# Read-out tables of an S5 layer formed beside the attention and kept in DRAM, with fixed bias buffers and gate stores on another queue

## The chip, the cores and the metric

The kernel runs on one core of a Trainium2 chip. The metric is the device time of one execution in microseconds (us). The engines are TensorE (PE in the profile; its weight loads are PEld), VectorE (DVE), ScalarE (ACT), GpSimd (POOL) and SyncE (SP), which here only issues transfers. Each engine works through its own instructions in order.

## What is computed

A backbone of two layers over 256 latent tokens with a prefix of 256 context tokens, width 1024, float32. In each layer one input projection feeds three token mixers and three gates:

```
h  = rms_norm(x) * (1.0 + sc1) + sh1
hc = rms_norm(ctx) * (1.0 + csc1) + csh1
u, rk, rv, nk, nv, rq, rg, nq, gates = split_cols(h @ w_in[l], IN_SPLIT)
y_s5, y_s5_c = s5_mixer(u, cu, ...)
y_ret, y_ret_c = retention_mixer(...)
y_na = neighborhood_attention(heads(nq), heads(nk), heads(nv), k_na_c, v_na_c, na_rpb[l])
x = x + g1 * merge_branches(y_s5, y_ret, y_na, gates, ...)
...
x = x + g2 * swiglu(rms_norm(x) * (1.0 + sc2) + sh2, ...)
```

Layer 0 does all of this for both streams (512 tokens), layer 1 for the latent tokens. The S5 mixer is a state space model with 32 groups of 16 channels and 64 complex states per group, in both directions. What matters here is its read-out:

```
jnp.einsum('ghp,blgp->blgh', c_re, x_re) - jnp.einsum('ghp,blgp->blgh', c_im, x_im)
```

## The kernel before

**Weights.** The weights stream from DRAM in chunks of 512 KB, in the order in which they are needed (`wraw`, L375, issued by SyncE into four raw buffers). ScalarE casts each chunk to a rounded copy (L385), VectorE subtracts this copy from the chunk and so gets the rest (L386), and each product of the network is three matmuls, L391 to L393 (`mm3`; L875 to L877 for the modulation). These are called weight matmuls below; 24 of them belong to a 128-column piece of weights over 512 tokens.

**Layer 0 around the change.** `weave` runs one generator as the main one and steps the others between its pieces, and so writes the program in an interleaved order; the scheduler of the framework then fixes the order on each engine. Buffers come from a hand-managed arena `F` that hands out space round robin, or from its top on request, so the arena's state decides what a new buffer overwrites and waits for. The sequence is: the attention's projections of the first half with the S5 input side; those of the second half with the S5 scan (`s5_scan`), the attention of the first half (`attn`) and modulation; then the gates with the attention of the second half; then, after the swap buffer is freed, more gates with the S5 read-out (`s5_out`); then the branch projections and retention, which begins with transposes at L1543.

**The S5 parts.** A sequence is cut into 32 chunks of 16 tokens. The scan runs on GpSimd over the states between chunks: 63 steps, each of two products (L1101) and two sums (L1104, L1105) on 128 x 64 elements, each step depending on the one before. Its tail exchanges two halves of the states through the buffer `swap`: two transfers on GpSimd's queue (L1111, L1112) and two copies (L1113, L1114).

The read-out needs tables per block of 8 groups, four blocks in a layer. `_prods` forms g on VectorE with six instructions over 128 x 1152 elements (L747, L748 products, L749 sum; twice, once per direction). `s5_kwin` multiplies g on TensorE by a window (L1158, called KWIN below, 16 matmuls), copies and corrects the result (L1162 to L1167) and stores it to DRAM as kws (L1171); `s5_t` loads it back in another layout as T, with four transfers (L1145). Then 48 matmuls (L1223, called OUT below) give the output: a third of them multiply by T and two thirds, with the scanned states, by g. Layer 0 does all of this inside `s5_out`; layer 1 forms its tables early, beside the FFN of layer 0 (`s5_kwins`), keeps g in DRAM as gsp and loads g and T back block by block (`s5_back`).

**Attention.** Scores, softmax, transposed scores (L1382, copied from PSUM by L1406 on ScalarE), values (L1410). Each head pair loads two bias tables (L1392), which ScalarE negates (L1393), into buffers from the arena.

**Gates.** TensorE forms a gate tile, ScalarE takes its tanh (L1668), and GpSimd's queue stores it to DRAM as tgs (L1671); SyncE loads it back later (L1687).

## Time and profile before

| | |
|---|---|
| median of three executions | 1570.82 us (1569.39 to 1572.18) |
| profiled execution: its time, its span | 1570.71 us, 1568.9 us |
| TensorE busy | 1500.3 us (96% of the span) |
| VectorE, ScalarE, GpSimd busy | 980.2, 631.9, 235.4 us |
| mean granted TensorE clock | 0.978 of full |
| read from and written to DRAM | 225.96 and 16.12 MB |

TensorE stands still for less than 5% of the span; its busy time also holds stretches in which the granted clock is at its lower level. An engine's idle time costs nothing unless TensorE waits for that engine, directly or through a chain.

### The profile page before, as it was taken

The page shows a single profiled execution, that of the slowest core. Times are in us where ns is not written, and L with a number is a line of the kernel's source. Part 1 is how long each engine was busy: PE and PEld are TensorE (multiplying, and loading weights), DVE is VectorE, ACT ScalarE, POOL GpSimd, SP SyncE. Part 2 cuts the span into 40 slices and gives each one's busy share as a digit, 9 for nine tenths or more (in the row PEclk, how much of TensorE's full clock was granted, in tenths as well). Part 3 has the DMA queues.
Part 4 walks back from the last instruction along what each step waited for, and adds up shares of the span by engine and source line. Part 5 has one row for each costly group of instructions (what it writes and reads, how often), then busy time and mean ns, then how long its engine had stood idle before and what let it go on. Part 6 is the DMA issues. An engine that isn't in the chain of part 4 may idle for free.

```text
span 1568.9 us, 25526 instructions
## 1 busy us (share of the span) xinstructions
PE 1500.3 (96%) x10066; PEld 1273.3 (81%) x10066; DVE 980.2 (62%) x1729; ACT 631.9 (40%) x1139; POOL 235.4 (15%) x620
## 2 busy tenths in 40 slices
PE   7899999969999999999999999999998999999997
PEld 6776677748887888787887788898777999899997
DVE  6683435466445587587699973732654776666566
ACT  4544444213522334332332322444644345453443
POOL 5205782000000000000000000006991000000000
PEclk9999999989999999999999999999999999999999
DMA  9423345644333323454565562432223786555552
GB/s 372 145 88 108 102 151 180 209 152 144 122 112 95 125 93 122 162 187 142 166 225 196 204 199 64 168 102 80 93 91 112 241 294 202 201 176 187 175 186 97
DMA packets 78584, 245.91 MB, mean 157 GB/s; under 512 B 9088, under 2 KB 22912, under 8 KB 76672
## 3 DMA queue, kind: packets, MB, share of 16 engines
q1 hardware_dynamic: 76864, 237.92, 46.3%
q0 software_dynamic: 1600, 6.36, 1.3%
q8 instruction: 79, 1.29, 0.3%
q14 instruction: 41, 0.34, 0.1%
HBM read 225.96 MB, written 16.12 MB: 154 GB/s over the span
## 4 chain that ended last, share of the span: by engine, by line
PE 70%; issue 8%; POOL 8%; DMA 7%; DVE 4%; ACT 1%; SPq 1%; POOLq 0%; DVEq 0%; ACTq 0%
PE psall L391 20%; PE psall L393 20%; PE psall L392 19%; DMA fa<-in_wst_dram 4%; POOL fa L1101 3%; POOL fa L1105 2%; POOL fa L1104 1%; PE psall L524 1%; PE psall L875 1%; PE psall L876 1%; DMA fa<-in_nabias_dram 1%; PE psall L877 1%; PE psall L1223 1%; PE psall L1582 1%; DMA fa<-fa 1%
## 5 line engine op out<-in xcount | busy, mean ns | idle before, releaser
L391 PE MATMUL psall<-ra 128*128 128x256 f32 (+1 forms) x2122 | 713.9, 340 | 9.3 <-DVE fa L1164 3.2
L393 PE MATMUL psall<-ra 128*128 128x256 f32 (+1 forms) x2122 | 707.6, 336 | 2.9 <-DVE ra L386 2.9
L392 PE MATMUL psall<-ra 128*128 128x256 f32 (+1 forms) x2122 | 710.1, 336 | 0.0
L386 DVE TENSOR_TENSOR ra<-fa,ra 128x1024 fp32r<-128x1024 f32 (+1 forms) x284 | 342.9, 1210 | 295.0 <-ACT ra L385 287.4
L385 ACT CAST ra<-fa 128x1024 fp32r<-128x1024 f32 (+1 forms) x284 | 293.7, 1037 | 560.6 <-PE psall L392 326.2
L391 PEld LDWEIGHTS psall<-ra 128*128 128x128 f32 x2122 | 402.7, 191 | 67.1 <-issue 11.7
L393 PEld LDWEIGHTS psall<-ra 128*128 128x128 f32 x2122 | 404.5, 191 | 46.9 <-DVE ra L386 3.9
L392 PEld LDWEIGHTS psall<-ra 128*128 128x128 f32 x2122 | 405.3, 191 | 39.8 <-issue 1.1
L1101 POOL TENSOR_TENSOR fa<-fa 128x64 f32<-128x64 f32 x252 | 87.4, 368 | 137.9 <-ACT fa L1069 128.3
L1050 POOL MEMSET fa<- 128x32 f32 x2 | 0.3, 126 | 691.0 <-DVE ra L834 691.0
L568 DVE SCALAR_TENSOR_TENSOR fa<-fa 128x1024 f32<-128x1024 f32 x70 | 87.2, 1277 | 9.2 <-DMA fa<-in_wst_dram 9.0
L875 PE MATMUL psall<-ra 128*128 128x512 f32 x192 | 78.4, 422 | 4.1 <-ACT ra L833 3.8
L876 PE MATMUL psall<-ra 128*128 128x512 f32 x192 | 77.5, 404 | 3.8 <-DVE ra L386 3.8
L877 PE MATMUL psall<-ra 128*128 128x512 f32 x192 | 74.1, 402 | 0.0
L1706 DVE SCALAR_TENSOR_TENSOR fa<-psall,fa 128x256 f32<-128x256 f32 x96 | 43.0, 477 | 46.4 <-PE psall L393 46.0
L875 PEld LDWEIGHTS psall<-ra 128*128 128x128 f32 x192 | 43.7, 230 | 13.0 <-ACT ra L833 4.9
L1105 POOL TENSOR_TENSOR fa<-fa 128x64 f32<-128x64 f32 x126 | 52.6, 417 | 9.8
L876 PEld LDWEIGHTS psall<-ra 128*128 128x128 f32 x192 | 44.5, 232 | 9.3 <-DVE ra L386 4.4
L1104 POOL TENSOR_TENSOR fa<-fa 128x64 f32<-128x64 f32 x126 | 48.0, 381 | 0.0
L877 PEld LDWEIGHTS psall<-ra 128*128 128x128 f32 x192 | 43.3, 232 | 5.6 <-issue 0.2
L748 DVE TENSOR_TENSOR fa<-fa 128x1024 f32<-128x1024 f32 (+1 forms) x32 | 40.2, 1283 | 7.2 <-DMA fa<-in_s5c_dram 7.2
L407 ACT CAST ra<-fa 128x512 fp32r<-128x512 f32 (+1 forms) x52 | 26.5, 509 | 44.6 <-DVE fa L1772 32.1
(244 smaller groups left out, 1409.4 us busy)
## 6 DMA issues: line engine op xcount, KB each, us to landing
fa<-in_wst_dram SPq DMA_DIRECT2D x364, 512.0 KB
fa<-in_wst_dram SPq DMA_DIRECT2D x16, 384.0 KB
gsp<-fa SPq DMA_DIRECT2D x4, 1152.0 KB
fa<-gsp SPq DMA_DIRECT2D x4, 1152.0 KB
xsp<-fa SPq DMA_DIRECT2D x2, 2048.0 KB
tgs<-fa POOLq DMA_DIRECT2D x16, 256.0 KB, 4.2
fa<-kws SPq DMA_DIRECT2D x32, 128.0 KB
fa<-tgs SPq DMA_DIRECT2D x16, 256.0 KB
```

Source lines behind the costliest of these rows:

```text
L385: nc.scalar.copy(hi[:, :n], t[:, :n])
L386: nc.vector.tensor_tensor(out=lo[:, :n], in0=t[:, :n], in1=hi[:, :n].bitcast(F32), op=ALU.subtract)
L391: mm(out, wh, xh, start=start, stop=False)
L392: mm(out, wh, xl, start=False, stop=False)
L393: mm(out, wl, xh, start=False, stop=stop)
L568: nc.vector.scalar_tensor_tensor(out=acc[s].ap, in0=t, scalar=c, in1=acc[s].ap, op0=ALU.mult, op1=ALU.add)
L875: mm(o, xh, hi[:, ws], start=(kk == 0), stop=False)
L876: mm(o, xh, lo[:, ws], start=False, stop=False)
L877: mm(o, xl, hi[:, ws], start=False, stop=(kk == 7))
L1101: e.tensor_tensor(out=t[:, i], in0=at(pf, pr), in1=tab[:, i * 64:(i + 1) * 64].rearrange("p (r d g) -> p r d g", r=2, d=2), op=ALU.mult)
L1104: e.tensor_tensor(out=at(cf, cr), in0=at(cf, cr), in1=t[:, 0], op=ALU.add)
L1105: e.tensor_tensor(out=at(cf, cr), in0=at(cf, cr), in1=mk(T[s % 2], 96, [[-32, 2], [16, 2], [1, 16]]), op=ALU.add)
```

## The change

Layer 0's tables are formed as layer 1's already are. `s5_kwins(0, True)` takes one buffer of 4480 columns from the arena's top, makes a small arena of its own in it, and forms g and the window there; it is woven into the second half of the attention's projections and the gates that follow. g goes to DRAM (gsp has eight tiles now) and `s5_out` of both layers loads g and T back. Four bias buffers of 384 columns are taken from the top for the whole attention of a layer. The gate stores move from GpSimd's queue to ScalarE's.

```diff
@@ layer 0
+            kw = self.s5_kwins(0, True)
             e_in = chain(*(g for blk in range(4) for g in (self.s5_e(0, b2, blk), self.s5_in(0, blk))))
             weave(self.m_na(l, 0, na), (e_in, 3))
             self.log_gamma(self.s5in[:, 192:208])
-            weave(self.m_na(l, 1, na), (self.s5_scan(l), 18), (self.attn(l, 0, na), 4), (self.take(ada, 5), 1))
-            weave(self.gates(l, 0, None), (self.attn(l, 1, na), 1.6), (self.take(ada, 5), 0.5))
+            weave(self.m_na(l, 1, na), (self.s5_scan(l), 18), (self.attn(l, 0, na), 4), (self.take(ada, 5), 1),
+                  (self.take(kw, 4), 1))
+            weave(self.gates(l, 0, None), (self.attn(l, 1, na), 1.6), (self.take(ada, 5), 0.5), (kw, 0.5))
             self.swap.free()
             weave(self.gates(l, 2, None), (self.s5_out(l, self.yslot[1]), 2), (self.take(ada, 5), 0.5))
@@ s5_kwins
-    def s5_kwins(self, l):
-
-        nc = self.nc
+    def s5_kwins(self, l, own=False):
+
+        nc, F = self.nc, self.F
+        if own:
+
+            buf = F.alloc(4480, "kwins", top=True)
+            F = Arena(buf.ap, 4480, "kwins")
         for blk in range(4):
-            gb, gv = self.s5_g(l, blk)
-            yield
-            self.s5_kwin(l, blk, gv)
-            nc.sync.dma_start(self.gsp[blk], gb.ap)
+            gb, gv = self.s5_g(l, blk, F)
+            yield
+            self.s5_kwin(l, blk, gv, F)
+            nc.sync.dma_start(self.gsp[l * 4 + blk], gb.ap)
             gb.free()
             yield
+        if own:
+            buf.free()
@@ s5_out
-        back = self.s5_back(0) if last else None
+        back = self.s5_back(l, 0)
         for blk in range(4):
-            if last:
-                gb, T = back
-                gv = self.g_view(gb)
-                back = self.s5_back(blk + 1) if blk < 3 else None
-                yield
-            else:
-                gb, gv = self.s5_g(l, blk)
-                yield
-                self.s5_kwin(l, blk, gv)
-                yield
-                T = F.alloc(1024, "T")
-                self.s5_t(l, blk, T)
-                yield
+            gb, T = back
+            gv = self.g_view(gb)
+            back = self.s5_back(l, blk + 1) if blk < 3 else None
+            yield
@@ m_na, attn
             self.nvb = F.alloc(2048, "na", top=True)
+            self.biases = [F.alloc(384, "bias", top=True) for _ in range(4)]
...
-                bias.append(F.alloc(384, "bias"))
+                bias.append(self.biases[m * 2 + h])
...
-            for h in range(2):
-                bias[h].free()
...
         if half == 1:
             self.nvb.free()
+            for b in self.biases:
+                b.free()
@@ gates
-                self.nc.gpsimd.dma_start(self.tgs[gi * 8 + mt], t.ap)
+                self.nc.scalar.dma_start(self.tgs[gi * 8 + mt], t.ap)
```

The scheduler moves more than the diff shows. Below are the engines' orders at three places; line numbers of the changed kernel are two higher than before from the S5 part on (L1166 for L1164, L1160 for L1158, L1103 for L1101), and L1222 is its OUT.

On VectorE, between the attention's second projections and its softmax, beside the scan, the order before was this (L1329, L1330, L1339, L1341: softmax; L408: the rest of a split):

```order
L1339 RECIPROCAL fa<-fa 128x2
L1330 ISA fa<-psall,fa 128x256
L1330 ISA fa 128x1
L1341 TENSOR_SCALAR fa<-fa 128x512 x2
L386 TENSOR_TENSOR ra<-fa,ra 128x1024
L408 TENSOR_TENSOR ra<-psall,ra 128x512
L386 TENSOR_TENSOR ra<-fa,ra 128x1024
L408 TENSOR_TENSOR ra<-psall,ra 128x512
```

At the same place of the changed kernel the table products stand between them:

```order
L748 TENSOR_TENSOR fa<-fa 128x1152
L386 TENSOR_TENSOR ra<-fa,ra 128x1024
L1330 ISA fa<-psall,fa 128x256
L1330 ISA fa 128x1
L749 TENSOR_TENSOR fa<-fa 128x8x144
L1338 TENSOR_TENSOR fa<-fa 128x2
L748 TENSOR_TENSOR fa<-fa 128x1152
L1339 RECIPROCAL fa<-fa 128x2
L1341 TENSOR_SCALAR fa<-fa 128x512 x2
L408 TENSOR_TENSOR ra<-psall,ra 128x512
L386 TENSOR_TENSOR ra<-fa,ra 128x1024
L747 TENSOR_TENSOR fa<-fa 128x8x144 x2
```

All 24 products of the four blocks have moved there, between the casts of weight matmuls 336 and 504 of layer 0's stream, where the scan runs on GpSimd; twelve L386 stand in the same stretch.

On GpSimd, in the scan, the gate stores stood between the steps:

```order
L1101 TENSOR_TENSOR fa<-fa 128x64 x2
L1104 TENSOR_TENSOR fa<-fa 128x2x2x16
L1671 DMA tgs<-fa 128x512
L1105 TENSOR_TENSOR fa<-fa 128x2x2x16
L1101 TENSOR_TENSOR fa<-fa 128x64 x2
```

In the changed kernel GpSimd's order has no L1671; on ScalarE each stands behind its tanh. Here is ScalarE's order at the end of the attention's second half, with the cast of the weight chunk that SyncE loads behind the first T (next fence) at its head:

```order
L385 CAST ra<-fa 128x1024
L1668 ACTIVATE fa<-psall 128x512
L1671 DMA tgs<-fa 128x512
L1406 COPY fa<-psall 128x512 x2
L534 COPY fa<-psall 128x256
L1349 ACTIVATE fa<-psall,fa 128x256 x4
```

On SyncE's queue in the changed kernel, the T loads of block 0 (L1147) wait for both swap transfers (DMASW) and the last copy of the scan's tail (Pool), because this T lies in the freed swap buffer; five weight chunks, T of block 1 and g of block 0 (L1138) are behind them:

```order
L1187 DMA gsp<-fa 128x2304 [waits DMAHW2_49,DVE_49]
L1147 DMA fa<-kws 128x2x128 [waits DMASW1_49,DMASW0_49,Pool_49]
L1147 DMA fa<-kws 128x2x128 [waits DMAHW4_49]
L1147 DMA fa<-kws 128x2x128 [waits DMAHW5_49]
L1147 DMA fa<-kws 128x2x128 [waits DMAHW6_49]
L375 DMA fa<-in_wst_dram 128x1024 [waits DMAHW0_49,DVE_49]
L375 DMA fa<-in_wst_dram 128x1024 [waits DMAHW2_49,DMAHW1_49,DVE_49]
L375 DMA fa<-in_wst_dram 128x1024 [waits DMAHW4_49,DMAHW0_49,DVE_49]
L375 DMA fa<-in_wst_dram 128x1024 [waits DMAHW5_49,PE_49]
L375 DMA fa<-in_wst_dram 128x1024 [waits DMAHW7_49,DMAHW6_49,PE_49]
L1147 DMA fa<-kws 128x2x128 [waits DMAHW7_49,PE_49]
```

TensorE's order in the changed kernel, just ahead of weight matmul 577, has the last KWIN (L1160), the attention's values L1410 that wait for L1406, and the first four OUT matmuls, whose right side is that T:

```order
L524 MATMUL psall<-fa 32x256 x7
L1160 MATMUL psall<-fa 32x128 x11
L1410 MATMUL psall<-fa 64x128
L1160 MATMUL psall<-fa 32x128 x5
L1410 MATMUL psall<-fa 64x128 x7
L538 MATMUL psall<-fa 128x128 x2
L1222 MATMUL psall<-fa 32x8x16 x4
L391 MATMUL psall<-ra 128x512
```

Before, the first OUT matmuls stood behind weight matmul 716, and all KWIN and OUT lay between 600 and 850.

## Rows read from the trace of the kernel before

**Rows 1.** Part 4 of the page: shares of the chain that ended last.

```profile
PE 70%; issue 8%; POOL 8%; DMA 7%; DVE 4%; ACT 1%; SPq 1%; POOLq 0%; DVEq 0%; ACTq 0%
```

**Rows 2.** Waits of TensorE, 316 to 360 us: total, times, longest.

```profile
PE psall L1158 <- DVE fa L749: 7.0, 2, 5.4
PE psall L1223 <- DMA fa<-kws: 3.8, 4, 2.5
PE psall L391 <- DVE fa L1164: 3.0, 1, 3.0
```

**Rows 3.** Windows: busy us (instructions) of PE, PEld, DVE, ACT, POOL; clock; DMA share; GB/s.

```profile
328.00:336.00 8.00, 2.59 (x11) 1.50 (x10) 5.12 (x5) 0.00 (x0) 0.00 (x0) 0.76 0.50 163
336.00:344.00 8.00, 3.42 (x34) 2.63 (x34) 6.34 (x8) 1.65 (x4) 0.00 (x0) 0.50 0.52 160
344.00:352.00 8.00, 4.96 (x46) 3.24 (x44) 4.96 (x10) 1.67 (x3) 0.00 (x0) 0.89 0.30 85
352.00:360.00 8.00, 7.66 (x105) 6.13 (x106) 1.28 (x2) 0.37 (x1) 0.00 (x0) 0.79 0.51 175
1188.00:1192.00 4.00, 3.42 (x16) 3.42 (x17) 3.91 (x7) 0.00 (x0) 0.00 (x0) 0.50 0.29 86
```

**Rows 4.** Timeline of TensorE: start, duration, instruction, idle before it.

```profile
263.42 0.48 PE L391 MATMUL psall<-ra 128*128 128x512 f32 x1
263.73 0.40 PE L392 MATMUL psall<-ra 128*128 128x512 f32 x1
263.96 0.40 PE L393 MATMUL psall<-ra 128*128 128x512 f32 x1
...
347.04 1.12 PE L1158 MATMUL psall<-fa 128*32 128x128 f32 x32
...
454.11 0.60 PE L1543 MATMUL psall<-fa 128*128 128x128 f32 x4
```

**Rows 5.** Timeline of GpSimd: the scan of layer 0 and its tail.

```profile
132.93 0.61 POOL L1101 TENSOR_TENSOR fa<-fa 128x64 f32<-128x64 f32 x2 [82.90 <-ACT fa L1069]
...
134.30 0.61 POOL L1101 TENSOR_TENSOR fa<-fa 128x64 f32<-128x64 f32 x2
...
237.31 0.32 POOL L1105 TENSOR_TENSOR fa<-fa 128x64 f32<-128x64 f32 x1
...
242.20 0.57 POOL L1671 DMA_DIRECT2D tgs<-fa  x1 [3.18 <-ACT fa L1668]
...
246.93 1.94 POOL L1114 COPY fa<-fa 64x2112 f32<-64x2112 f32 x1
```

**Rows 6.** Groups of GpSimd, 132 to 250 us: busy, mean ns, idle before.

```profile
L1671 POOL DMA_DIRECT2D tgs<-fa x6 | 3.7, 617 | 8.6 <-ACT fa L1668 8.6
```

**Rows 7.** Timeline of VectorE and GpSimd at 149 us.

```profile
149.25 1.35 DVE L386 TENSOR_TENSOR ra<-fa,ra 128x1024 fp32r<-128x1024 f32 x1 [2.64 <-ACT ra L385]
...
149.60 1.46 POOL L1101 TENSOR_TENSOR fa<-fa 128x64 f32<-128x64 f32 x2
```

**Rows 8.** Timeline of VectorE: products at the old place.

```profile
330.88 1.36 DVE L748 TENSOR_TENSOR fa<-fa 128x1152 f32<-128x1152 f32 x1 [5.12 <-DMA fa<-in_s5c_dram]
...
339.82 2.63 DVE L747 TENSOR_TENSOR fa<-fa 128x1152 f32<-128x1152 f32 x2 [1.66 <-ACT fa L1122]
```

**Rows 9.** Timeline of SyncE's queue: the window loads of a block.

```profile
347.41 2.54 SPq L1145 DMA_DIRECT2D fa<-kws  x4
```

**Rows 10.** Chain that ended last, 130 to 365 us: start, us, what.

```profile
232.62 4.68 DMA fa<-in_wst_dram
...
348.76 3.53 DMA fa<-kws
```

**Rows 11.** Timeline of ScalarE: a cast and the copies L1406.

```profile
185.63 1.05 ACT L385 CAST ra<-fa 128x1024 fp32r<-128x1024 f32 x1 [5.32 <-issue]
...
188.75 1.07 ACT L1406 COPY fa<-psall 128x512 f32<-128x512 f32 x2 [1.57 <-PE psall L1382]
```

**Rows 12.** Waits of TensorE in the whole span.

```profile
PE psall L1556 <- DVE fa L1548: 7.2, 1, 7.2
```

More of the change, by code (lines that the diff above doesn't have):

```diff
@@ L259, in run @@
         self.xsp = dr.tile([P, 4096], F32, name="xsp")
-        self.gsp = dr.tile([4, P, 2304], F32, name="gsp")
+        self.gsp = dr.tile([NL * 4, P, 2304], F32, name="gsp")
         self.F = Arena(fa, NF, "F")
@@ L669, in s5_prep_small, with swapped @@
         self.dump("pw", PW)
-    def swapped(self, name, c0, n):
-        a, b = self.F.alloc(n, name), self.F.alloc(n, name)
+    def swapped(self, name, c0, n, F):
+        a, b = F.alloc(n, name), F.alloc(n, name)
         src = self.I[name]
@@ L690, in s5_tables @@
                 nc.scalar.copy(dst, src)
-        w1, w2 = self.swapped("s5b", l * 1024, 1024)
+        w1, w2 = self.swapped("s5b", l * 1024, 1024, F)
         nc.scalar.mul(w2.ap, w2.ap, self.sgn[:, 0:1])
@@ L733, in log_gamma, with _prods @@
         self.dump("lg", lg)
-    def _prods(self, dst, A, B, c0, l, blk, nb, op):
+    def _prods(self, dst, A, B, c0, l, blk, nb, op, F):
         n0 = nb - 1
@@ L739, in _prods @@
         for d in range(2):
-            tmp = self.F.alloc(nb * 128, "prod")
+            tmp = F.alloc(nb * 128, "prod")
             eng = self.nc.vector
@@ L758, in s5_e @@
         e = F.alloc(2048, "e")
-        self._prods(e.ap, self.tabs[l][1].ap, b2.ap, blk * 256, l, blk, 8, ALU.add)
+        self._prods(e.ap, self.tabs[l][1].ap, b2.ap, blk * 256, l, blk, 8, ALU.add, F)
         yield
@@ L1115, in s5_scan, with s5_g @@
         yield
-    def s5_g(self, l, blk):
-        gb = self.F.alloc(2304, "g")
-        c1, c2 = self.swapped("s5c", l * 1024 + blk * 256, 256)
+    def s5_g(self, l, blk, F):
+        gb = F.alloc(2304, "g")
+        c1, c2 = self.swapped("s5c", l * 1024 + blk * 256, 256, F)
         self.nc.scalar.mul(c1.ap, c1.ap, self.sgn[:, 1:2])
-        self._prods(gb.ap, c1.ap, c2.ap, 0, l, blk, 9, ALU.subtract)
+        self._prods(gb.ap, c1.ap, c2.ap, 0, l, blk, 9, ALU.subtract, F)
         c1.free()
@@ L1130, in g_view, with s5_back @@
         return gb.ap.rearrange("p (q r d n) -> p q r d n", q=4, r=2, d=2)
-    def s5_back(self, blk):
+    def s5_back(self, l, blk):
         nc = self.nc
         gb, T = self.F.alloc(2304, "g"), self.F.alloc(1024, "T")
-        nc.sync.dma_start(gb.ap, self.gsp[blk])
-        self.s5_t(1, blk, T)
+        nc.sync.dma_start(gb.ap, self.gsp[l * 4 + blk])
+        self.s5_t(l, blk, T)
         return gb, T
@@ L1145, in s5_t, with s5_kwin @@
             self.nc.sync.dma_start(Tv[:, q], src)
-    def s5_kwin(self, l, blk, gv):
-        nc, F = self.nc, self.F
+    def s5_kwin(self, l, blk, gv, F):
+        nc = self.nc
         kw = F.alloc(480, "kw")
```

## The prediction

> **What bounds the kernel now.** I read the chain that ended last first: TensorE holds 70% of it, GpSimd 8%, transfers 7%, VectorE 4% [rows 1]. So the time moves only where TensorE stands still, or runs at half clock after standing still. The waits of TensorE in 316 to 360 us show where layer 0 forms its read-out tables: 7.0 us for products of VectorE (L749), 3.8 us for the window loads from kws, 3.0 us for the small sums behind the window (L1164) [rows 2]. The windows of that stretch show the second half of the cost: the granted clock falls to 0.50 to 0.89 [rows 3]. Width less busy time times clock is what a window loses: 6.0, 6.3, 3.6 and 2.0 us, 17.9 us between 328 and 360. This is all that the change can win at that place.
>
> **What the change moves.** Its 24 products, 64 KWIN matmuls, loads and stores are the same in number. They leave this stretch and run beside the attention. Added are four stores and four loads of g.
>
> *The old place.* The 17.9 us go. The KWIN matmuls of one block take 1.1 us [rows 4], 4 x 1.05 = 4.2 us, and are earlier now. As the order shows, the first four OUT matmuls now stand 576 weight matmuls into layer 0's stream. In the kernel before, the weight matmul at 263.42 us is the 589th and retention's first transposes (L1543) start at 454.11 [rows 4]: 190.7 us. With 12 weight matmuls more (0.23 us apart [rows 4], 2.8 us), without the 17.9 lost us and the 4.2, TensorE needs 171.4 us from weight matmul 577 to L1543. By itself it would reach that matmul at 263.4 - 2.8 + 4.2 = 264.8. If nothing else held it, L1543 would start at 436.2 instead of 454.1.
>
> *The new place.* VectorE's products now lie inside the scan of GpSimd, and the scan ends the chain of what comes next. A scan step takes 1.37 us undisturbed, the scan began at 132.93 and its last step ended at 237.63: 104.7 us for 63 steps, where 63 x 1.365 = 86.0 [rows 5]. Part of the surplus are the gate stores on GpSimd's queue: 3.7 us of issues and 8.6 us of waits for ScalarE, less 0.6 and 3.2 of a store behind the scan, so 8.5 us [rows 5, 6]. The change takes these away. The other part is VectorE: where L386, which subtracts two arrays of SBUF, ran at 149.25, the pair L1101 took 1.46 us instead of 0.61 [rows 5, 7]. I read the ten L386 in the scan like this; the eight beside working GpSimd instructions each cost it 0.86 to 1.09 us, 0.98 on average, that is their own length less about 0.25 us. Instructions that read one input from SBUF did nothing like it. A product has two inputs in SBUF too and takes 1.31 to 1.36 us [rows 8], so by the same reading it holds the scan for about 1.08 us. The trace shows no product beside the scan. The bounds are 0 and its whole length: 24 products cost 0 to 32 us, and I take 24 x 1.08 = 25.9, because L386 is the same operation on the same number of elements to within an eighth.
>
> The Trainium skill ("SBUF — State Buffer", section "Who interferes with whom") says that a VectorE instruction with two SBUF inputs and a GpSimd instruction that reads SBUF exclude each other for the whole instruction. The trace agrees (0.98 of 1.23 us lost per L386); by the rule alone the products would cost their full 32 us, which puts everything below 6 us later, by the row 25.9.
>
> Scan after: it starts some 1.9 us later, at 134.8 (the order puts nine weight matmuls and three scores ahead of its last input, 2.1 + 0.9 us, and one cast a product earlier, 1.1). Then 86.0 + 0.4 for a copy, 2.2 unexplained as before, 12 L386 x 0.98 = 11.8, products 25.9. Its end is 261.1 (bounds 235 and 268).
>
> *What waits for the scan's end.* The order shows that the first T loads of SyncE's queue wait for the two swap transfers and the last copy of the scan's tail, since T now lies where the swap buffer lay. The tail took 11.2 us [rows 5], and needs it again: 272.3. The four issues take 2.5 us [rows 9]: 274.9. Behind them in the same queue stands the next weight chunk, which landed 4.7 us after its release in the kernel before [rows 10]: 0.4 for the issue and 4.7 give 280.0 (window loads alone took 3.5). ScalarE's queue has the cast of this chunk (1.05 us) ahead of tanh, gate store and the two copies L1406 (1.07) for the attention's turned scores [rows 11]: about 282.6 for the first. TensorE has L1410, which waits for these copies, then L538 and the four OUT matmuls ahead of weight matmul 577. I allow 2.4 us: 285.0. Against its own 264.8 that is a wait of some 20 us, which replaces the waits of the old place. Everything that TensorE loses earlier in the attention, such as KWIN waiting for a product or the bias loads, disappears in it as long as it is under 20 us.
>
> After it TensorE has half clock for a while: at the one comparable place, after 7.2 us of standing still in layer 1, the four us from 1188 had 3.42 busy at 0.50 [rows 3], a loss of 2.3; I take 2.5. L1543 then starts at 285.0 + 171.4 + 2.5 = 458.9, which is 4.8 us later than before.
>
> *The rest.* Fixed bias buffers may spare waits for bias loads: one in the attention, now hidden by the long wait, and one at layer 1's start, where the order still has the loads behind the store of x. I take 1 us as gain, with bounds of 0 and 3. The gate stores cost ScalarE 16 issues, 0.6 us each by GpSimd's rows [rows 6], 10 us spread over 200; ScalarE is idle most of that time, and the cover ends only at casts that TensorE awaits. The wait of layer 1 for the same tail (7.2 us [rows 12]) is behind the same number of weight matmuls as before, and stays. The extra 9.4 MB of g in DRAM move under a DMA share of about a half [rows 3].
>
> Sum: 4.8 - 1 = +3.8 on the profiled execution, whose span of 1568.9 us lies in a time of 1570.71; the median, 1570.82, is the same within 0.1. That gives 1574.5 us.
>
> **Rivals.** *The products don't hold up the scan* (bound 0). Then the scan ends at 235, T's wait is over by 259, before TensorE comes at 264.8, and L1543 moves by -17.9: with the 1 us of the rest, 1552 us. For it: no product beside the scan is shown. Against it: eight of eight L386.
>
> *They hold it half.* 0.5 us each: scan end 247, matmul 577 at 271, L1543 at 445: -9 to -10, 1561 us. The boundary below which there is no wait at all is a scan end of 241.
>
> *SyncE's queue starves what follows* (slower). While T waits, five chunks, T of block 1 and g of block 0 stand behind it, 2.5 + 0.5 + 1.2 = 4.2 MB. At the 160 GB/s of this stretch [rows 3] that is 26 us, and TensorE then holds weights for 72 matmuls, 17 us. The wait grows by up to 9 us: 1583 us. It decides where the burst moves below some 250 GB/s. Against it: those 160 GB/s came with a DMA share of 0.5 [rows 3], so about twice as much is to be had.
>
> *The order is not what decides*: the OUT matmuls could be as late as before because g comes back late from DRAM. Then the loss of the old place is only moved to loads, near 4 us per block at most, and the time lies within the same span as the forecast.
>
> **How the numbers follow.** The forecast (scan end 255 to 267, 1568 to 1581 us) has 0.54, no hold-up 0.14, half 0.12, starving 0.20. A measurement of this kernel can tell about 0.2%, 3.1 us. Faster: 0.14 + 0.12 + 0.04 of the forecast's low end = 0.30. Same, 1567.7 to 1574.0: 0.21 of the forecast's middle. Slower: its upper part, 0.29, and starving, 0.20. The range reaches from no hold-up, 1552, to 1582, and leaves out most of the starving.
>
> **What would show it.** Right: the scan of layer 0 ends near 261 and each product beside it lengthens a GpSimd instruction by about a us; no gate store in it; TensorE waits 15 to 22 us near 265 to 283 for a copy of ScalarE that stands behind a cast that awaits a weight chunk; no idle at 330 to 350 us of the old kind. Wrong: a scan of under 108 us, or OUT matmuls that start near 265 without a wait, or the wait's end more than 5 us from 24 us behind the scan's last step.

## The result: slower, and by more than forecast

The changed kernel takes 1594.82 us (median of 6 runs, 1592.36 to 1599.62); the kernel before took 1573.53 in the same comparison. The ratio is 1.0138, 95% interval 1.0114 to 1.0162. The forecast was 1574.5 with a range to 1582. The profiled execution of the changed kernel took 1594.24 us, with a span of 1592.5 against 1568.9. The direction was the forecast's likelier one; the size was not, and no case that I had written down ends there.

The first view is again the chain that ended last, in part 4 of the page of the changed kernel. It answers to [rows 1].

```profile
PE 73%; POOL 10%; DVE 5%; issue 5%; DMA 5%; ACT 2%; SPq 0%; DVEq 0%; ACTq 0%; POOLq 0%
```

GpSimd's share grew from 8 to 10%, that of transfers fell from 7 to 5. So the scan is on the path for longer, which I had forecast, and the question is who waits for it. Next come the waits of TensorE over the whole span of the changed kernel (total, times, longest):

```profile
PE psall L391 <- ACT fa L1668: 19.8, 1, 19.8
PE psall L1543 <- ACT fa L1485: 12.7, 1, 12.7
PE psall L391 <- ACT ra L385: 8.2, 8, 3.8
...
PE psall L393 <- DVE ra L386: 5.0, 3, 3.5
...
PE psall L1160 <- DVE fa L749: 2.5, 2, 1.3
```

The waits at the old place [rows 2] are gone. In their place stand a wait of 19.8 us for ScalarE's tanh of a gate (L1668), one of 12.7 us for ScalarE's copies L1485 ahead of layer 1's retention, where layer 1 had 7.2 before [rows 12], and 3.8 and 3.5 us of waits for weights. None of these is the wait that I forecast, which was for a copy L1406.

**Layer 0.** The timeline of the changed kernel around the first wait, by engine (start, duration, instruction, idle before it and what ended it):

```profile
222.24 0.59 ACT L1406 COPY fa<-psall 128x512 f32<-128x512 f32 x1
249.84 0.62 ACT L1088 ACTIVATE fa<-fa 128x32 f32<-128x32 f32 x4 [27.01 <-POOL fa L1103]
250.38 1.03 ACT L385 CAST ra<-fa 128x1024 fp32r<-128x1024 f32 x1
251.31 0.59 ACT L1668 ACTIVATE fa<-psall 128x512 f32<-128x512 f32 x1
251.93 0.33 ACTq L1671 DMA_DIRECT2D tgs<-fa  x1
...
231.00 1.11 PE L1160 MATMUL psall<-fa 128*32 128x128 f32 x32
251.95 0.80 PE L391 MATMUL psall<-ra 128*128 128x512 f32 x1 [19.84 <-ACT fa L1668]
...
251.44 1.23 DVE L386 TENSOR_TENSOR ra<-fa,ra 128x1024 fp32r<-128x1024 f32 x1 [28.79 <-ACT ra L385]
...
249.49 0.59 POOL L1103 TENSOR_TENSOR fa<-fa 128x64 f32<-128x64 f32 x2
...
250.44 0.32 POOL L1107 TENSOR_TENSOR fa<-fa 128x64 f32<-128x64 f32 x1
...
263.08 2.83 POOL L1116 COPY fa<-fa 64x2112 f32<-64x2112 f32 x1
...
296.15 0.43 PE L1222 MATMUL psall<-fa 128*32 128x128 f32 x8
...
459.88 0.60 PE L1543 MATMUL psall<-fa 128*128 128x128 f32 x4
```

Read it from ScalarE. L1088 fills the scan's table of coefficients, four instructions of 0.2 us each, and these four are for the scan of *layer 1*. The table lies in a fixed buffer (`scan_tmp`) that layer 0's scan reads until its last step. So ScalarE stands from 222.8 to 249.8 for the last product of that scan at 249.49. Its queue is in order: behind L1088 are a cast of weights, and tanh of a gate. VectorE has no cast to work on and stands 28.8 us; TensorE uses up what it has and stands 19.8. T is loaded behind the scan's tail, as forecast, but now TensorE is itself so late that it doesn't wait for it: the first OUT matmuls (L1222) start at 296.15, when it comes to them. In the kernel before, the same four instructions wait for 1.8 us, just behind the last products of a scan that ended at 237.63:

```profile
236.70 0.63 ACT L1086 ACTIVATE fa<-fa 128x32 f32<-128x32 f32 x4 [1.79 <-POOL fa L1101]
```

The scan of the changed kernel itself ends at 250.8 us, ten before the forecast: it runs for 115.4 us, and only 19 of the 24 products and 8 of the L386 fall into it, because VectorE stands still behind ScalarE for its last part.

The windows of the changed kernel (columns as in [rows 3]) show the stretch, the way from the first OUT matmul to retention, and layer 1's wait:

```profile
220.00:240.00 20.00, 12.12 (x123) 9.05 (x119) 1.40 (x1) 2.43 (x4) 17.80 (x57) 0.91 0.22 67
240.00:260.00 20.00, 8.05 (x25) 6.20 (x26) 8.56 (x13) 4.75 (x17) 10.78 (x34) 0.58 0.38 85
...
296.00:460.00 164.00, 164.00 (x1106) 132.66 (x1105) 74.05 (x108) 60.62 (x95) 0.00 (x0) 1.00 0.57 191
...
1188.00:1200.00 12.00, 0.00 (x0) 0.00 (x0) 0.11 (x2) 1.92 (x5) 5.59 (x7) 0.67 0.40 90
1200.00:1220.00 20.00, 18.57 (x128) 16.15 (x129) 8.36 (x15) 11.88 (x27) 0.01 (x1) 0.77 0.16 53
```

TensorE is busy for 8 of the 20 us from 240, at a granted clock of 0.58, and VectorE for 1.4 of the 20 us from 220. From 296 to 460 TensorE runs without a gap at full clock.

**Layer 1.** The timeline of the changed kernel at the start of retention:

```profile
1198.04 0.82 ACT L1567 COPY fa<-fa 64x256 f32<-64x256 f32 x2 [14.97 <-POOL fa L1115]
1198.88 2.05 ACT L1485 COPY fa<-psall 128x512 f32<-128x512 f32 x4
...
1200.50 1.12 PE L1543 MATMUL psall<-fa 128*128 128x128 f32 x4 [12.71 <-ACT fa L1485]
```

L1567 writes a buffer of retention that lies where the swap buffer lay, so it waits 15.0 us for the copies of the scan's tail. Before, VectorE's L1548 waited there, beside the others, and TensorE could still do its transposes L1543 (at 1177.46):

```profile
1187.24 1.29 DVE L1548 TENSOR_TENSOR fa<-psall,fa 128x512 f32<-128x512 f32 x2 [9.73 <-POOL fa L1114]
```

Now ScalarE waits, and has the copies for L1543 behind it: TensorE stands 12.7 us, with nothing done from 1188 to 1200.

**The account.** Spans can be split at retention's transposes L1543: at the first of layer 0 and the last of layer 1, which are the first and the last start of that line in each profile. The rest are differences:

| us of the span | before | after | difference |
|---|---|---|---|
| start to the first L1543 of layer 0 | 454.1 | 459.9 | +5.8 |
| to the last L1543 of layer 1 | 723.7 | 741.3 | +17.6 |
| to the end | 391.1 | 391.3 | +0.2 |

Of the 17.6, 12.7 are layer 1's wait and 7.4 idle time of TensorE in the FFN (the feed-forward part, `swiglu`) at 860 to 900 us (9.55 against 2.11, with the waits of 3.8 and 3.5 for weights in it); the remainder is 2.5 shorter. The last row is even although before has its 7.2 us of [rows 12] in it: after loses as much to half clock (0.77 in 1200 to 1220) and small waits.

### The profile page after: what moved, and what is told of

It reads as the page before. It is cut to its first block, busy times and chain, and to the rows that moved or that the text cites. A ratio compares the mean times of both kernels' runs of the same rounds, so it can differ in the third digit from the quotient of the medians.

```text
span 1592.5 us, 25516 instructions
## 1 busy us (share of the span) xinstructions
PE 1495.6 (94%) x10066; PEld 1274.3 (80%) x10066; DVE 988.6 (62%) x1729; ACT 633.2 (40%) x1139; POOL 246.8 (15%) x604
## 4 chain that ended last, share of the span: by engine, by line
PE 73%; POOL 10%; DVE 5%; issue 5%; DMA 5%; ACT 2%; SPq 0%; DVEq 0%; ACTq 0%; POOLq 0%
PE psall L391 20%; PE psall L393 20%; PE psall L392 20%; POOL fa L1103 5%; DMA fa<-in_wst_dram 4%; POOL fa L1107 3%; POOL fa L1106 2%; PE psall L875 2%; PE psall L876 1%; PE psall L877 1%; PE psall L524 1%; ACT ra L385 1%; DVE ra L386 1%; PE psall L1582 1%; DVE fa L568 1%
## 5 line engine op out<-in xcount | busy, mean ns | idle before, releaser
L391 PE MATMUL psall<-ra 128*128 128x256 f32 (+1 forms) x2122 | 711.5, 340 | 35.5 <-ACT fa L1668 19.8
L386 DVE TENSOR_TENSOR ra<-fa,ra 128x1024 fp32r<-128x1024 f32 (+1 forms) x284 | 345.2, 1217 | 337.1 <-ACT ra L385 325.0
L391 PEld LDWEIGHTS psall<-ra 128*128 128x128 f32 x2122 | 403.1, 192 | 91.9 <-ACT fa L1668 20.1
L1103 POOL TENSOR_TENSOR fa<-fa 128x64 f32<-128x64 f32 x252 | 101.7, 424 | 139.0 <-ACT fa L1071 129.3
L1107 POOL TENSOR_TENSOR fa<-fa 128x64 f32<-128x64 f32 x126 | 52.8, 419 | 9.9
L1106 POOL TENSOR_TENSOR fa<-fa 128x64 f32<-128x64 f32 x126 | 52.5, 416 | 0.0
L748 DVE TENSOR_TENSOR fa<-fa 128x1024 f32<-128x1024 f32 (+1 forms) x32 | 41.0, 1287 | 9.8 <-DMA fa<-in_s5c_dram 5.9
L747 DVE TENSOR_TENSOR fa<-fa 128x1024 f32<-128x1024 f32 (+1 forms) x32 | 40.5, 1305 | 8.3 <-ACT fa L1124 6.6
```

The lines of the kernel that those rows point to most:

```text
L386: nc.vector.tensor_tensor(out=lo[:, :n], in0=t[:, :n], in1=hi[:, :n].bitcast(F32), op=ALU.subtract)
L391: mm(out, wh, xh, start=start, stop=False)
L1103: e.tensor_tensor(out=t[:, i], in0=at(pf, pr), in1=tab[:, i * 64:(i + 1) * 64].rearrange("p (r d g) -> p r d g", r=2, d=2), op=ALU.mult)
L1106: e.tensor_tensor(out=at(cf, cr), in0=at(cf, cr), in1=t[:, 0], op=ALU.add)
L1107: e.tensor_tensor(out=at(cf, cr), in0=at(cf, cr), in1=mk(T[s % 2], 96, [[-32, 2], [16, 2], [1, 16]]), op=ALU.add)
```

## The experiments

Theory: each layer has a wait behind its scan. In layer 0 it is ScalarE's table for the next layer, and hidden behind it a second one, for the T loads, which must wait because T lies in the freed swap buffer. In layer 1 it is the same kind of buffer reuse. Rivals: the products' hold on the scan is the loss itself; moving the tables is what costs; one of the two side edits (biases, gate stores) does it.

Medians of all runs, with the interval of the ratio to the kernel before in the same comparison (1570.3 to 1571.1 us there), and the split of the profiled span as above. A profiled execution is one of them: that of e3 is 3.6 us slower than its median, that of e7 5.5 us faster, the others lie within 2.7 us.

| kernel | us | ratio, 95% interval | to L1543 of layer 0 | to that of layer 1 | to the end |
|---|---|---|---|---|---|
| e1_late_table | 1583.63 | 1.0080 (1.0052 to 1.0108) | 449.0 | 739.7 | 390.7 |
| e8_swap_kept_layer0 | 1563.09 | 0.9947 (0.9927 to 0.9966) | 437.1 | 733.7 | 392.6 |
| e2_swap_kept_both | 1545.67 | 0.9836 (0.9804 to 0.9868) | 439.0 | 720.9 | 385.3 |
| e14_both_edits_again (the same) | 1544.24 | 0.9827 (0.9809 to 0.9844) | 433.6 | 722.7 | 385.9 |
| e3_before_late_table_swaps_kept | 1561.90 | 0.9942 (0.9916 to 0.9968) | 453.4 | 726.7 | 383.7 |
| e9_all_but_tables_waits_gone | 1561.34 | 0.9931 (0.9912 to 0.9951) | 446.0 | 726.9 | 385.9 |
| e5_bias_only | 1571.67 | 1.0000 (0.9981 to 1.0018) | 437.5 | 741.4 | 390.7 |
| e6_gates_only | 1565.14 | 0.9955 (0.9941 to 0.9970) | 449.1 | 723.4 | 390.8 |
| e13_change_without_tables | 1567.04 | 0.9978 (0.9965 to 0.9992) | 442.0 | 732.5 | 390.1 |
| e7_tables_only | 1567.43 | 0.9977 (0.9957 to 0.9997) | 445.9 | 723.3 | 390.9 |
| e4_one_input_products | 1529.33 | 0.9732 (0.9704 to 0.9760) | 428.0 | 716.8 | 385.4 |
| e10_broadcast_products | 1533.02 | 0.9752 (0.9732 to 0.9771) | 429.1 | 716.8 | 386.9 |

Line numbers of these kernels differ from those of the changed kernel by one or two, either way; L1544 is its L1543, L1411 its L1410, L1407 its L1406, L1486 its L1485, L1568 its L1567, L1223 and L1224 its L1222, L1108 its L1107. In e13, L1086 is its L1088 and L1101 its L1103; in e7, L1374 is the scores' L1375, L1391 and L1392 are the load of a bias and its negation, L1667 and L1670 a gate's tanh and its store.

### The table of layer 1's scan, filled later

The edit to the changed kernel: layer 1's table is filled behind the last copy of its S5 input, and so far behind layer 0's scan.

```diff
-                    nc.scalar.copy(dst, src)
+                    self.s5_last = nc.scalar.copy(dst, src).ins
...
-        for i in range(4):
-            nc.scalar.mul(tab[:, i * 32:(i + 1) * 32]...
+        with self.tc.issue_after(self.s5_last) if l else nullcontext():
+            for i in range(4):
+                nc.scalar.mul(tab[:, i * 32:(i + 1) * 32]...
```

> The changed kernel with one edge more: the four ScalarE instructions that fill the scan's coefficient table for layer 1 (L1088 of the changed kernel) may not be issued before layer 1's last scan input. Nothing else in the order differs. Theory A (ScalarE's queue stood still for 27.0 us behind these four, which wait for the last step of layer 0's scan, and TensorE lost 19.8 us there; behind it waits the T load of my prediction): the wait goes, the scan then runs beside all 24 products again and ends near 261 us, TensorE waits for T and the weight chunk behind it, and the first OUT matmul starts near 284 us instead of 295.9. About 11 us less, 1584 us. Theory B (the T loads alone set the time, the ScalarE wait only fills the same hole): 1592 to 1597 us. Theory C (the ScalarE wait was the whole loss): about 22 us less, 1573 us.

It took 1583.63 us, 11.2 less than the changed kernel (9 by the two ratios; they come from different comparisons, and L1543 of layer 0 is 10.9 earlier). Its waits of TensorE and a piece of its timeline:

```profile
PE psall L1544 <- ACT fa L1486: 12.8, 1, 12.8
PE psall L1411 <- ACT fa L1407: 8.4, 3, 7.2
...
281.15 0.69 PE L1411 MATMUL psall<-fa 128*64 128x128 f32 x2 [7.24 <-ACT fa L1407]
```

The wait of 19.8 us is gone. What is left in layer 0 is the wait that the prediction described, for the copy that stands behind the cast of a chunk that SyncE issues behind T; it is 7.2 us long, and the first OUT matmuls start at 285.3, where the prediction's steps give about 284. So L1088 on ScalarE's queue is shown as the cause of the first wait, which covered the second. Taking 19.8 us of waiting away gives back some 11 because 7.2 of the second appear. Layer 1's wait is untouched, 12.8.

### The swap buffer kept, in layer 0 and in both layers

Two more edits, each one moved line: the swap buffer is freed only behind the S5 read-out (layer 0), so that T lies elsewhere, and only behind retention (layer 1).

```diff
# layer 0, on top of the late table (e8)
-            self.swap.free()
             weave(self.gates(l, 2, None), (self.s5_out(l, self.yslot[1]), 2), (self.take(ada, 5), 0.5))
+            self.swap.free()
# layer 1, on top of both (e2, e14)
-            self.swap.free()
             self.m = F.alloc(8 * n, "m", top=True)
             weave(self.branch(l, 2, self.yna, 0), (self.retention(l), 2.5))
+            self.swap.free()
```

> As the kernel with the late table, and the swap buffer of layer 0 is given back to the arena behind the read-out instead of ahead of it, so that T of block 0 lies elsewhere and waits for no part of the scan. Theory A: no wait before the first OUT matmul, which starts near 265 us; OUT with the scanned states comes some 10 us later and finds the scan's tail done at about 272. Some 18 us less than with the late table alone, near 1566 us. If the T load is no second wall: no change against the kernel with the late table.

> As the kernel before this one in the list, and the swap buffer of layer 1 too is given back only after retention, so that neither kd nor qt (L1548, L1567) overwrites it. Theory A: TensorE's wait of 12.7 us at retention's first transposes of layer 1, which comes from copies of ScalarE that wait for the scan's tail, goes, and with it about 3 us at half clock: 14 to 16 us less, near 1551 us, faster than the kernel before by over 1%. If layer 1's wait is covered by another one of the same length behind it: under 4 us less.

> The whole change with the late table and both swap buffers kept once more, for the comparison on the same chip: 1542 to 1549 us.

The steps were 20.5 us for layer 0's buffer and 17.4 for layer 1's, and 1545.67 and 1544.24 in the end. That is 47 to 51 us less than the changed kernel (by the ratios or by the medians) and some 25 less than the kernel before, from edits that change no arithmetic and only say when a table is filled and where a buffer lies. It is the best version of this case that computes what the reference does. The first waits of TensorE in e2, and lines that start retention and OUT (ns of one: min, median, max; first and last start):

```profile
PE psall L335 <- DMA fa<-in_ctx_dram: 6.5, 1, 6.5
PE psall L875 <- ACT ra L833: 5.2, 1, 5.2
PE psall L391 <- ACT fa L1350: 3.9, 1, 3.9
PE psall L1161 <- DVE fa L749: 3.6, 2, 1.8
```

```profile
L1223 PE MATMUL psall<-fa x576: 272/273/332, 280.9 to 1258.2; 128*32 128x128 f32 x192
...
L1544 PE MATMUL psall<-fa x8: 272/272/273, 439.0 to 1159.9; 128*128 128x128 f32 x8
```

No wait over 6.5 us is left, the first two belong to the program's start and to the modulation, and the L1544 of both layers run at full clock (272 ns; the changed kernel's median is 347). Layer 0's retention starts at 439.0 and 433.6, where the prediction's "if nothing else held it" gives 436.2.

The step of e8 holds more than the wait of 7.2 us: L1544 of layer 0 is 11.9 us earlier, 10.7 of it less idle time from 120 us on (9.3 against 20.1). The order moved too: the first OUT matmuls stand behind 600 weight matmuls in e8, e2 and e14, no longer behind 576, and start at 279.6 in e8, where I had expected 265. That the time, 1563.09, came near the 1566 that I had expected is in part luck. Another 6.0 us come from the stretch up to layer 1, where TensorE's idle time in the FFN fell from 9.6 to 2.4 us. The edit does nothing there. The changed kernel, e1 and e5 have those 7 to 10 us of idle time, e3 and e9 3.6 and 5.2, the kernel before and the others at most 2.5, and e4 and e10 below, whose products are shorter, none; why isn't settled.

### The same two edits on the kernel before

The edit is that of e2, made to the kernel before.

```diff
+        with self.tc.issue_after(self.s5_last) if l else nullcontext():
...
# both lines self.swap.free() moved as in e2
```

> The kernel before, with the two edits of the kernel with both swap buffers kept (late table for layer 1, swap buffers given back later) and nothing of the change. It tells what of that kernel's 25 us comes from the edits alone. Theory A: the edits take away layer 1's wait (7.2 us and about 2 at half clock) and nothing in layer 0, where the order has no long wait on the scan: near 1561 us, so that the change itself is worth some 15 us once its waits are gone. If the edits are the whole gain and the change is worth nothing: near 1546 us.

It took 1561.90 us, 9 less than before. The split shows where: 7.4 in the last stretch, since layer 1's wait of 7.2 is gone. Layer 0 stays at 453.4, with the waits at the old place. So the two edits alone don't give the 25 us; they are worth 9 us on the kernel before and some 50 on the changed one.

### Is the move of the tables worth anything?

Everything but the tables, with the two edits, is to be set beside e14.

```diff
# on the kernel before
+            self.biases = [F.alloc(384, "bias", top=True) for _ in range(4)]
-                bias.append(F.alloc(384, "bias"))
+                bias.append(self.biases[m * 2 + h])
-                self.nc.gpsimd.dma_start(self.tgs[gi * 8 + mt], t.ap)
+                self.nc.scalar.dma_start(self.tgs[gi * 8 + mt], t.ap)
# and the edits of e2
```

> The kernel before with fixed bias buffers, gate stores on ScalarE's queue, the late table and both swap buffers kept, but with the tables of layer 0 formed inside the read-out as before. Against the kernel with all of the change and the same two edits it tells what the move of the tables is worth once its waits are gone. Theory A (the bias buffers alone had already emptied the old place: retention of layer 0 began at 437 us there, at 439 in the kernel with everything): 1541 to 1549 us, the same as with the tables moved. Theory D (the move of the tables is what wins, 16 us between the kernel before and the whole change with the same edits): 1555 to 1562 us.

1561.34 against 1544.24 in the same comparison: moving the tables gives 17 us once nothing waits at the scan. The split puts 12.4 of the 16.6 us between the two profiles into layer 0 up to retention and 4.2 into the stretch after it, none behind it. It isn't idle time: from 120 us to retention TensorE stands still for 11.3 us in e9 and 10.8 in e14, and the number of matmuls of each kind is the same, so the same matmuls keep TensorE busy for longer. The groups of the two kernels from 80 us to retention (first e9, then e14: busy us, mean ns, idle before):

```profile
L1377 PE MATMUL psall<-ra 64*128 64x512 f32 (+1 forms) x96 | 20.3, 390 | 2.2 <-DVE ra L408 2.2
L1224 PE MATMUL psall<-fa 128*32 128x128 f32 x384 | 15.3, 275 | 2.9 <-DMA fa<-kws 2.7
```

```profile
L1376 PE MATMUL psall<-ra 64*128 64x512 f32 (+1 forms) x96 | 17.0, 361 | 0.0
L1223 PE MATMUL psall<-fa 128*32 128x128 f32 x384 | 11.7, 274 | 0.0
```

The same 384 OUT matmuls hold TensorE for 15.3 us in one kernel and 11.7 in the other, and the same 96 scores for 20.3 and 17.0. In e9 TensorE still waits for window loads in the midst of OUT (2.7 us), and its clock in 320 to 360 us is 0.91, where e14 has 1.00 (first e9, then e14):

```profile
320.00:360.00 40.00, 34.76 (x277) 25.07 (x275) 27.56 (x37) 10.10 (x17) 0.00 (x0) 0.91 0.43 133
```

```profile
320.00:360.00 40.00, 40.00 (x197) 32.02 (x187) 18.09 (x24) 12.53 (x24) 0.00 (x0) 1.00 0.59 200
```

In windows of 40 us from 120 us to retention the granted clock of the two differs only there. So the clock is worth at most 0.09 of 40 us, 3.6 of the 12.4. Most of the rest are matmuls that hold TensorE longer at full clock; why they do isn't shown.

### Each part alone

The three parts of the change, each alone on the kernel before, and the two side edits together.

```diff
# e5: fixed bias buffers alone
+            self.biases = [F.alloc(384, "bias", top=True) for _ in range(4)]
-                bias.append(F.alloc(384, "bias"))
+                bias.append(self.biases[m * 2 + h])
# e6: gate stores alone
-                self.nc.gpsimd.dma_start(self.tgs[gi * 8 + mt], t.ap)
+                self.nc.scalar.dma_start(self.tgs[gi * 8 + mt], t.ap)
# e13: e5 and e6 together;  e7: the changed kernel with both undone
```

> The kernel before with the fixed bias buffers alone. Its order has the table of layer 1's scan 524 weight matmuls into layer 0 (528 before), but in layer 1 the copies to qt now stand on ScalarE's queue behind the scan's tail, as in the changed kernel. Theory A: layer 0 as before within 2 us, in layer 1 a wait of 12 to 13 us at retention's first transposes in place of the 7.2: 5 to 9 us slower, 1575 to 1580 us. If the longer wait in layer 1 comes from another part of the change: the same as before within 3 us.

> The kernel before with the gate stores on ScalarE's queue alone. The scan of layer 0 loses its 8.5 us of stores and waits and ends near 229 to 231 us; the table for layer 1's scan moves up to 504 weight matmuls, which TensorE reaches at about the same time, so ScalarE waits at most 2 us for it. Same as before within 3 us, 1568 to 1573 us. If stores on ScalarE's queue delay its casts: slower by 3 to 10 us.

> The kernel before with the tables' part of the change alone: biases from the arena, gate stores on GpSimd's queue. The order has the table for layer 1's scan at 503 weight matmuls, T of block 0 outside the swap buffer, and layer 1's retention as before. Theory A: the scan, now with the products and the gate stores, lasts past 260 us, ScalarE stands some 25 to 30 us behind it and TensorE about 20: layer 0 loses as much as in the changed kernel or a little less, layer 1 does not: 1582 to 1590 us. If the products alone do no harm: 1550 to 1570 us.

> The change without its tables: fixed bias buffers and gate stores on ScalarE's queue, no edits. Theory A (the 27 us of ScalarE's wait came from the scan growing by the products while the order, which has layer 1's scan table at 504 weight matmuls here and at 477 in the changed kernel, reckons with a short scan): ScalarE waits under 3 us for the scan here; layer 0 gains some 16 us as with the bias buffers alone, layer 1 loses most of it at the copies behind the scan's tail: 1562 to 1571 us. If gates and biases together already make the long wait: 1585 us or more.

e5 came out at 1571.67, no change, where I had expected a loss. The reason is a surprise: the bias buffers alone shift layer 0's retention from 454.1 to 437.5, as far as the whole change was meant to. TensorE's idle time in 300 to 440 us fell from 14.3 to 3.0 us, though the tables are formed where they were. They come earlier there: the KWIN of the last block starts at 331.2 us, 347.0 before. And layer 1 gives all of it back: 741.4 instead of 723.7, with the wait for L1486 (11.3 us) and 5.0 more idle in the FFN. Every kernel with fixed bias buffers and without layer 1's late free has that wait ahead of retention's transposes: after 12.7, e1 12.8, e8 12.8, e5 11.3, e13 13.0. Those without fixed bias buffers (before, e6, e7) have the 7.0 to 7.2 us at the later matmul. So the longer wait of layer 1 comes from the bias buffers, not from the tables. Its line in e5 is the one of the changed kernel:

```profile
1175.79 0.82 ACT L1568 COPY fa<-fa 64x256 f32<-64x256 f32 x2 [13.53 <-POOL fa L1113]
```

e6 gave 5 to 6 us where I had expected nothing. The scan took 97.4 us, 7.3 less than in the kernel before, so the prediction's 8.5 us for the stores was about right; layer 0's retention came 5.0 earlier.

e7, the tables alone, is at 1567.43: a small gain, where I had expected a loss of 12 to 19 us. Here is the wait of ScalarE for the scan in e7, then in e13:

```profile
254.28 0.63 ACT L1088 ACTIVATE fa<-fa 128x32 f32<-128x32 f32 x4 [9.89 <-POOL fa L1103]
```

```profile
229.65 0.23 ACT L1086 ACTIVATE fa<-fa 128x32 f32<-128x32 f32 x1 [4.66 <-POOL fa L1101]
```

With the tables alone the fill of the table stands behind 503 weight matmuls and waits for 9.9 us; with the two side edits alone it stands behind 504, and the scan is short, so it waits 4.7. With all three it stands behind 477 and the scan is long: 27.0. Neither part has the long wait for the scan by itself. But e7 has a long wait of another kind, and it makes ScalarE reach the table late, at 244 us and not at 223:

```profile
205.84 0.80 POOL L1670 DMA_DIRECT2D tgs<-fa  x1 [0.32 <-issue]
...
SPq L1391 <- DMA tgs<-fa: 15.5, 1, 15.5
...
210.99 0.52 ACT L1392 ACTIVATE fa<-fa 128x384 f32<-128x384 f32 x1 [12.45 <-DMA fa<-in_nabias_dram]
...
PE psall L1374 <- ACT fa L1334: 12.6, 1, 12.6
```

The tanh of the first gate is done at 190.7, but its store stands among the scan's steps on GpSimd's queue and is issued at 205.8. A bias load on SyncE's queue waits 15.5 us for this store, so its buffer lies where the gate's tile lay. ScalarE waits for the bias, and TensorE stands 12.6 us at 212. Fixed bias buffers should take this chain away, and so should gate stores on ScalarE's queue; neither of the two was run alone with the tables. So the 9.9 us of e7 are no measure of the table's place in the order alone. The parts' effects don't add up: e13 gains 4 us, e7 gains 4, and both together lose 21.

### Does an instruction with one input hold the scan?

The products of e2, with one of their two inputs replaced by a constant (e4), and the same with the input that repeats each element 16 times (e10).

```diff
# e4, on e2
-            eng.tensor_tensor(out=o, in0=mk(P2, po, pd), in1=mk(A, wo, wd), op=ALU.mult)
+            eng.tensor_scalar(out=o, in0=mk(A, wo, wd), scalar1=0.5, scalar2=None, op0=ALU.mult)
# e10, on e2
+            eng.tensor_scalar(out=o, in0=mk(P2, po, pd), scalar1=0.5, scalar2=None, op0=ALU.mult)
# and likewise the second product and the sum
```

> As the kernel with both swap buffers kept, but each product of the tables reads one array of SBUF only (a multiplication with a constant of the same size): the tables hold other numbers and the output is not the reference's. Theory A (a VectorE instruction with two inputs in SBUF holds up GpSimd for about its length): layer 0's scan takes about 100 us instead of 124 to 127 with the true products; the time stays within 4 us of that kernel's, since nothing waits for the scan any more. If the products don't hold up the scan: the scan's length is the same in both within 3 us.

> As the kernel with one-input products, but each reads the table of powers with its 16-fold repeated elements instead of an array with a step of one; the tables hold other numbers. In the earlier kernel the one-input products ran in 0.76 us instead of 1.35 and still held the scan for 0.4 to 0.6 us each, so that it told length from inputs badly. If they take 1.2 us or more here: theory A expects no hold of the scan by them, a scan of 98 to 103 us and a time within 4 us of the kernel with true products. If one input holds as long as two: a scan of 122 to 126 us. If they run in 0.76 us again: near 110 us, as before.

In the changed kernel the products beside the scan read like this, VectorE's beside GpSimd's:

```profile
163.55 1.35 DVE L748 TENSOR_TENSOR fa<-fa 128x1152 f32<-128x1152 f32 x1
164.83 1.34 DVE L386 TENSOR_TENSOR ra<-fa,ra 128x1024 fp32r<-128x1024 f32 x1
...
163.38 0.32 POOL L1106 TENSOR_TENSOR fa<-fa 128x64 f32<-128x64 f32 x1
163.77 1.31 POOL L1107 TENSOR_TENSOR fa<-fa 128x64 f32<-128x64 f32 x1
165.16 1.47 POOL L1103 TENSOR_TENSOR fa<-fa 128x64 f32<-128x64 f32 x2
```

A sum that takes 0.32 us took 1.31 beside the product, and a pair of products 1.47 instead of 0.60 beside an L386. In e4, one of the table instructions, now with one input:

```profile
159.22 0.74 DVE L749 TENSOR_SCALAR fa<-fa 128x1152 f32<-128x1152 f32 x1
...
159.22 0.93 POOL L1108 TENSOR_TENSOR fa<-fa 128x64 f32<-128x64 f32 x1
```

With one input it takes 0.74 us instead of 1.35, and the scan's sum still loses 0.61. Most of e4's shortened products cost the scan 0.4 to 0.6 us each, and the scan took 109.6 us, where e2 has 124.4 and I had expected about 100; e10's took 108.1. Its time, 1529.33, was 16 us below e2 where I had expected at most 4. Both kernels shorten every product of the program, so their times say nothing on the hold, and since neither gave a one-input instruction of full length throughout, whether such an instruction would hold the scan for its whole length is open.

## Why the prediction was wrong

**What was right.** The old place is free of its waits. The products do hold the scan: in e2, where nothing else interferes, it ran from 135.74 to 260.15, 124.4 us, and the prediction's sum gives 126.3; its lengthenings add up to some 38 us where 11.8 + 25.9 = 37.7 were forecast. The tail and the T loads do make a wait that ends at the forecast time, once nothing hides it: the first OUT matmuls start at 285.3 in e1, against about 284. The gate stores cost the scan 7.3 us against 8.5, and ScalarE 0.33 us each rather than 0.6. The rivals "no hold-up" and "half" fell with the scan; SyncE's starving queue did not show, nor late g.

**The step that failed: "The rest".** It says that layer 1's wait "is behind the same number of weight matmuls as before, and stays", and gives the fixed bias buffers 1 us of gain with bounds of 0 and 3. From layer 0's retention to the end the changed kernel lost 17.8 us (1132.6 against 1114.8), where the step has -1: 18.8 of the 19.7 us between the forecast and the profiled execution. The position among the weight matmuls was the wrong thing to read. What counted was which engine waits there. The bias buffers moved the reuse of the swap buffer, and the wait with it, from VectorE's queue (L1548), which leaves TensorE work to go on with, to ScalarE's (L1567), which has that work's copies behind it. The kernel with the bias edit alone shows it (741.4 against 723.7 us), and freeing the swap buffer later removes it: from e8 to e2 the stretch with the wait is 12.8 us shorter and the last one 7.3. The part of the loss in the FFN, about 7 us, is shown by place only. The step was also too small the other way: in layer 0 the fixed bias buffers alone brought retention 16.6 us forward (e5), and with the tables and neither side edit TensorE stood 12.6 us behind a bias load (e7).

**A second failure that its opposite hid: "What waits for the scan's end".** The step followed only SyncE's queue. ScalarE's queue had an earlier customer of the scan, the next layer's table behind 477 weight matmuls, which I didn't look for. It cost 12 us at the first OUT matmul (296.2 against about 284), and e1, which moves it, gains 9 to 11 us in time. Yet retention started at 459.9, 1.0 from the forecast, because the way from the first OUT to it took 163.7 us, all of it busy at full clock, and not 174.9. That the two errors cancel is luck.

The forecast's split is off in the same sense where nothing waits. e14 reaches weight matmul 577 at 269.6 us (264.8 forecast) and needs 164.1 from there (171.4 forecast). Up to it, TensorE stands 5.1 us longer than in the kernel before up to the weight matmul at 263.42 (10.8 against 5.7 us, from 120 us on), in waits for softmax and products that the forecast had hidden in the long wait; and the KWIN matmuls took 6.2 us, not 4.2. Against that, the 577th weight matmul of the kernel before started at 258.7, 4.7 us ahead of the 589th and not 2.8, since other matmuls lie between the twelve. From there on, the kernel before needed 195.4 us, 31.4 more than e14; 5.8 of them are KWIN, so the old place gave back 25.6 us and not 17.9. TensorE's idle time there was 14.3 us, and about 5 went to a clock of 0.73 in 328 to 360 us; the rest are mostly the same matmuls, which took longer. The sum of both halves, 433.6, is within 3 us of the forecast 436.2, but the halves were mis-sized by 5 and 7 us, and it is luck that they cancel.

**What would have shown it.** The forecast said that a wait that doesn't end within 5 us of 24 us behind the scan's last step would prove it wrong; TensorE's long wait ended 1 us behind that step (251.95 against 250.8). Beforehand, the order of ScalarE's queue holds both waits: L1088 ahead of a cast in layer 0, and L1567 ahead of L1485 in layer 1.

**What stays open.** Why the FFN's idle time comes and goes; why the bias buffers alone empty the waits at the old place; and why the same matmuls take longer at full clock where the tables are formed inside the read-out (the kernel before, e9).

## What to carry to other kernels

When an edit makes some work longer, list every instruction on every in-order queue that waits for its end, in both layers, not only the consumer of its result: four instructions of 0.2 us that refill a small buffer for the next layer cost some 11 us here, because casts stood behind them. Buffers that are freed and reused across stages are such waits too, and where the waiting instruction stands on a queue (behind nothing, or ahead of the copies that TensorE needs next) can matter more than how long it waits. A change that fails can hold a gain: the same parts, with two lines moved and one table filled later, run at 0.983 of the kernel before, while none of the parts alone is worth more than 0.5%.

## What the runs showed of the hardware

An instruction of VectorE with a single SBUF input, 1152 elements in 0.74 to 0.76 us, still lengthens a GpSimd instruction beside it by 0.4 to 0.6 us (e4, e10), where I had taken two inputs to be the condition; the loss was again its own length less 0.13 to 0.35 us, as with two inputs (0.99 of 1.35 in the changed kernel). Short one-input instructions of the softmax did less: a GpSimd instruction beside L1341 (a multiplication of 512 elements by a scalar, 0.49 to 0.64 us) lost 0.1 to 0.3 us. The kernel before already showed this: beside L1341 and L1355 nine instructions of the scan lost 1.6 us together, most of the 2.2 that the prediction left unexplained.
